# A transformer block on one Trainium2 core: the split of q and k for five pairs of heads in operations of 128 rows, with the halves put in place by transfers

## The chip, the core and the metric

The kernel runs on one core of a Trainium2 chip. A core has a matrix engine (TensorE, PE in the profile, with its weight loads as PEld), a vector engine (VectorE, DVE), a scalar engine (ScalarE, ACT), GpSimd (POOL) and SyncE (SP), which here only issues transfers. Each engine works through its own instructions in the order of the program; engines wait for each other by semaphores. Transfers (DMA) are issued by SP, ACT or POOL and run on 16 DMA engines. The metric is the time of one execution on the device in microseconds.

## The reference

One block for 512 tokens of width 1024: a gated feed-forward, a mixer of two kinds of attention, a second gated feed-forward, and a gated embedding, each with norms. Only the mixer's attention matters here:

```python
u = rms_norm(h, g_mix_pre[i])
qkv = u @ w_in[i]
q_a, k_a, v_a, q_b, k_b, v_b = jnp.split(
    qkv, np.cumsum([W_SB, W_SB, W_SB, W_CH, W_CH])[:5].tolist(), axis=-1)
o_a = stick_breaking_attention(split_heads(q_a, H_SB), split_heads(k_a, H_SB),
                               split_heads(v_a, H_SB))
o_b = chunk_band_attention(split_heads(q_b, H_CH), split_heads(k_b, H_CH),
                           split_heads(v_b, H_CH), rel_bias[i])
```

There are eight heads of each kind, of dimension 64. Both kinds begin with the scores, q times k transposed, for blocks of 128 queries.

## The kernel before

Every float32 product is made of rounded operands: a value x is split into a high half, which is x rounded to the matrix engine's float32r format (`act.copy`), and a low half, x minus the high half (`dve.tensor_tensor` with subtract). A product is then the sum of high x high, high x low and low x high. Weights arrive in raw tiles (`wr`, by SP's transfers, L187), are split into `wh` and `wl` (L313 on ACT, L314 on DVE), and are used by `mm3` (L248 to L250).

The mixer is one software pipeline. TensorE's order is written by hand: a loop over 64 steps (L1050), each of which takes one block of 128 queries of one head, makes its scores (`z`, L887 and L888), turns the weights of three steps ago (`pt`, L937, split into `th` and `tl`, L313 and L314) and multiplies those of five steps ago with v (`po`, L951 and L952). Between them `fill` puts a number of products from a list of work: the projections to q and k (`pj`, in `project`), to v (`pv`), and later of the output. The order on the other engines is chosen by the scheduler from its own costs. The raw weights of this part are fetched five chunks ahead of their split.

Heads go in pairs, s = 0 to 7; in this text a pair is named by that number (pairs 0 to 3 are of the first kind, 4 to 7 of the second; in the program's names pair 4 g + i has the suffix g i, so `qd010` is tile qd0 of pair 4). The projection of a pair gives q and k for 128 rows, 64 per head: `top` is the pair's first head, `bot` the second. `qk_out` (L815) makes from them three kinds of tiles, two of each (0 for the first head, 1 for the second), all of 128 rows by 512 tokens, so that the three products of the scores are done in two products over 128 rows:

- `qd0`, `qd1`: the high half of the head's q, twice, in top and in bot;
- `ks0`: k's high half of the first head in top, its low half in bot; `ks1`: the second head's low half in top, its high half in bot;
- `ql0`, `ql1`: q's low half in the head's own rows, zeros in the others (a memset by POOL, L824).

`z` is qd times ks plus ql times ks. Each kind of tile has two buffers, so pair s takes those of pair s - 2. Except for q of pairs 0 to 3 the projections' result is first multiplied on DVE by a norm factor into a scratch tile `qkf` (L830 for q, L832 for k), which lies in one buffer under the tag `t3`. Then, for q and k each, ACT casts the two heads with one operation of 64 rows each (L835), DVE subtracts with one of 64 rows each (L842), and for q ACT issues two transfers that copy the high half to the other 64 rows (L837). For k the low half is written by the subtraction straight into the other head's rows.

Pairs 0 and 1 are projected ahead of the loop; `PLAN` (L56) orders the rest. The second kind of attention adds a bias tile (`bi`, L915, by SP) to the scores (`zbc`, L922). The first kind makes `fa` and `be` on ACT (L900, L901), masks them on POOL (L903), and scans and multiplies them on DVE into `a` (L906, L907).

## Time and profile before

| | |
|---|---|
| median of 3 runs | 1002.78 us (1001.17 to 1005.86) |
| the profiled execution, its own time | 1002.25 us |
| its span, from the first to the last instruction | 1000.5 us |
| busy: PE, DVE, ACT, POOL | 980.4, 775.3, 585.8, 134.5 us |
| transfers of L837, ACT's queue | 16 of 128 KB, 3.0 us from issue to landing (median) |
| biases of L915, SP's queue | 8 of 256 KB, 2.7 us (median) |

Times in the rows of a profile count from the start of the span. A row of a timeline shows its start, its length, the engine and line, the operation, the tiles as written<-read, their shapes, how many were merged, and in brackets how long the engine stood idle before it and what ended that. The three products of `mm3` show as L248, L249 and L250. In the views of transfers a row ends with the size and the median time from issue to landing.

### The profile page before, as it was taken

How to read it: one execution, taken by the hardware profiler on the slowest of the kernel's cores; microseconds unless marked ns; L12 is line 12 of the kernel's file. 1: busy time of each engine (PE TensorE's matmuls, PEld its weight loads, DVE VectorE, ACT ScalarE, POOL GpSimd, SP SyncE). 2: the span in 40 equal slices, each digit the busy share in tenths (PEclk: the TensorE clock that was granted, in tenths of full speed). 3: DMA queues.
4: the chain of work that ended last, by engine and by line, in shares of the span. 5: the costliest groups of instructions: out<-in, count | busy, mean ns of one | idle time of the engine just before them, and what ended most of it. 6: DMA issues, size and time to landing. Idle time of an engine off the chain costs nothing.

```text
span 1000.5 us, 18453 instructions
## 1 busy us (share of the span) xinstructions
PE 980.4 (98%) x7242; PEld 922.5 (92%) x7242; DVE 775.3 (77%) x1357; ACT 585.8 (59%) x979; POOL 134.5 (13%) x221
## 2 busy tenths in 40 slices
PE   9999999999999999999999999999999999999996
PEld 7889999999999999888898899899999999999885
DVE  6777787677667788999999767796776787676857
ACT  6446654564455467777789655565643664555563
POOL 0001112122210004343000000011122122210000
PEclk9999999999999999999999999999999999999999
DMA  7348888988896132313332402269789888975202
GB/s 280 102 106 189 170 188 183 207 181 177 211 191 206 60 82 88 89 61 102 99 89 92 139 10 65 61 142 204 149 186 204 181 169 212 195 180 185 64 1 85
DMA packets 44855, 139.71 MB, mean 140 GB/s; under 512 B 5216, under 2 KB 5600, under 8 KB 44768
## 3 DMA queue, kind: packets, MB, share of 16 engines
q0 software_dynamic: 14976, 50.34, 30.5%
q1 hardware_dynamic: 28368, 85.83, 25.3%
q10 hardware_dynamic: 1424, 2.36, 0.9%
q8 instruction: 57, 0.93, 0.4%
q14 instruction: 30, 0.25, 0.1%
HBM read 134.31 MB, written 2.10 MB: 136 GB/s over the span
## 4 chain that ended last, share of the span: by engine, by line
PE 75%; DMA 8%; DVE 8%; ACT 4%; issue 4%; POOL 0%; SPq 0%; DVEq 0%; POOLq 0%; ACTq 0%
PE f_a L248 7%; PE f_a L250 7%; PE f_a L249 7%; PE f_c L248 3%; PE f_c L250 3%; PE f_c L249 3%; PE pj L248 3%; PE pj L249 3%; PE pj L250 3%; DMA wy<-in_wst_dram 3%; DVE wl L314 2%; PE pt L937 2%; PE f_d L250 2%; PE f_d L249 2%; PE f_d L248 2%
## 5 line engine op out<-in xcount | busy, mean ns | idle before, releaser
L314 DVE TENSOR_TENSOR wl<-wx,wh 128x1024 fp32r<-128x1024 f32 (+1 forms) x104 | 118.3, 1139 | 39.6 <-ACT wh L313 38.7
L313 ACT CAST wh<-wx 128x1024 fp32r<-128x1024 f32 (+1 forms) x104 | 101.8, 985 | 68.1 <-DMA wx<-in_wst_dram 37.4
L314 DVE TENSOR_TENSOR wl<-wr,wh 128x1024 fp32r<-128x1024 f32 (+2 forms) x100 | 109.3, 1099 | 28.8 <-ACT wh L313 28.1
L313 ACT CAST wh<-wr 128x1024 fp32r<-128x1024 f32 (+2 forms) x100 | 94.3, 950 | 46.0 <-DMA wr<-in_wgu_dram 14.0
L223 POOL DMA_DIRECT2D wx<-in_wst_dram x54 | 47.1, 872 | 403.8 <-DVE wl L314 339.5
L313 ACT CAST wh<-wy 128x1024 fp32r<-128x1024 f32 (+1 forms) x52 | 51.4, 988 | 47.5 <-DMA wy<-in_wdst_dram 23.7
L314 DVE TENSOR_TENSOR wl<-wy,wh 128x1024 fp32r<-128x1024 f32 (+1 forms) x52 | 59.2, 1139 | 15.8 <-ACT wh L313 15.2
L248 PE MATMUL pj<-um_hi,wh 128*128 128x512 f32 (+1 forms) x160 | 56.7, 355 | 1.2 <-DVE f_f L658 1.1
L249 PE MATMUL pj<-um_lo,wh 128*128 128x512 f32 (+1 forms) x160 | 55.7, 348 | 0.1
L250 PE MATMUL pj<-um_hi,wl 128*128 128x512 f32 (+1 forms) x160 | 55.8, 348 | 0.0
L248 PE MATMUL f_a<-f_U6h,wh 128*128 128x256 f32 x144 | 40.0, 278 | 2.0 <-DVE f_x L599 1.3
L248 PE MATMUL f_a<-f_U0h,wh 128*128 128x256 f32 x144 | 40.0, 278 | 0.0
L249 PE MATMUL f_a<-f_U0l,wh 128*128 128x256 f32 x144 | 39.8, 277 | 0.0
L250 PE MATMUL f_a<-f_U0h,wl 128*128 128x256 f32 x144 | 39.8, 277 | 0.0
L248 PE MATMUL f_b<-f_U1h,wh 128*128 128x256 f32 x144 | 39.8, 277 | 0.0
L249 PE MATMUL f_b<-f_U1l,wh 128*128 128x256 f32 x144 | 39.8, 277 | 0.0
L250 PE MATMUL f_b<-f_U1h,wl 128*128 128x256 f32 x144 | 39.8, 277 | 0.0
L248 PE MATMUL f_c<-f_U2h,wh 128*128 128x256 f32 x144 | 39.8, 277 | 0.0
L249 PE MATMUL f_c<-f_U2l,wh 128*128 128x256 f32 x144 | 39.8, 277 | 0.0
L250 PE MATMUL f_c<-f_U2h,wl 128*128 128x256 f32 x144 | 39.8, 277 | 0.0
L248 PE MATMUL f_a<-f_U5h,wh 128*128 128x256 f32 x144 | 39.8, 277 | 0.0
L249 PE MATMUL f_a<-f_U5l,wh 128*128 128x256 f32 x144 | 39.8, 277 | 0.0
(461 smaller groups left out, 3851.3 us busy)
## 6 DMA issues: line engine op xcount, KB each, us to landing
wx<-in_wst_dram POOLq DMA_DIRECT2D x54, 512.0 KB, 5.7
wx<-in_wst_dram SPq DMA_DIRECT2D x18, 512.0 KB, 4.9
wy<-in_wst_dram SPq DMA_DIRECT2D x18, 512.0 KB, 5.8
wr<-in_wst_dram SPq DMA_DIRECT2D x18, 512.0 KB, 5.8
wy<-in_wst_dram POOLq DMA_DIRECT2D x18, 512.0 KB, 5.8
wx<-in_wdst_dram POOLq DMA_DIRECT2D x24, 384.0 KB, 5.5
wr<-in_wqk_dram SPq DMA_DIRECT2D x16, 512.0 KB, 3.7
wr<-in_wgu_dram SPq DMA_DIRECT2D x15, 512.0 KB, 4.2
```

The costliest lines, as they stand in the source:

```text
L223: pool.dma_start(out=r, in_=block, accum_op=ALU.add)
L248: pe.matmul(ps, hi, mh, start=start, stop=False, skip_group_check=skip)
L249: pe.matmul(ps, hi, ml, start=False, stop=False, skip_group_check=skip)
L250: pe.matmul(ps, lo, mh, start=False, stop=stop, skip_group_check=skip)
L313: a = act.copy(hi, src)
L314: b = dve.tensor_tensor(lo, src, hi.bitcast(F32), ALU.subtract)
L937: pe.transpose(pt[:, qi * P:(qi + 1) * P], aw[qi][:, (j - qi) * P:(j - qi + 1) * P], ident[:])
```

## The change

For pairs 2 to 6 (`2 <= 4 * g + i < 7`), q and k are cast by one operation of 128 rows each, into qd0 or ks0 whole, and subtracted by one operation of 128 rows. The low half goes back into the scratch tile, or, for q of pairs 2 and 3, where the source lies in PSUM, into a new tile under the same tag `t3`. Then `move`, a transfer on SP's queue of 64 rows, puts the halves in place: for q five (the second head's high half into both halves of qd1, the first head's over the second's in qd0, the low halves into ql0 and ql1), for k three (the second head's high half to ks1, its low half to ks1, the first head's low half over the second head's high half in ks0). The two transfers on ACT's queue go for these pairs. Pairs 0, 1 and 7 are as before, and so are all products.

```diff
             for r, other in enumerate((bot, top)):
                 pool.memset(ql[r][other, :].bitcast(F32), 0.0)
+            def move(dst, src):
+                nc.sync.dma_start(out=dst.bitcast(F32), in_=src.bitcast(F32))
+
             for j, ps in enumerate(pss):
                 src = ps
                 if g or j:
...
                 dst = ks if j else qd
+                if 2 <= 4 * g + i < 7:
+                    a, b = dst
+                    act.copy(a[:], src[:])
+                    lo = (src if g or j else tmp(f"qlf{g}{i}", 3))[:].bitcast(F32R)
+                    dve.tensor_tensor(lo, src[:], a[:].bitcast(F32), ALU.subtract)
+                    move(b[bot, :], a[bot, :])
+                    move(b[top, :], lo[bot, :] if j else a[bot, :])
+                    move(a[bot, :], lo[top, :] if j else a[top, :])
+                    if j == 0:
+                        move(ql[0][top, :], lo[top, :])
+                        move(ql[1][bot, :], lo[bot, :])
+                    continue
                 for r, (own, other) in enumerate(((top, bot), (bot, top))):
                     act.copy(dst[r][own, :], src[own, :])
```

The order on TensorE and on GpSimd is the same before and after. On SyncE's queue, this is what stands between the projection weights and the biases around pair 4 before (`wr` with its chunk's number, `bi` with the head's):

```order
L187 DMA wr137_5605<-in_wqk_dram 128x1024
L187 DMA wr138_5737<-in_wqk_dram 128x1024
L187 DMA wr139_5842<-in_wo_dram 128x1024
L915 DMA bi0_5817<-in_bias_dram 128x512
L915 DMA bi1_5968<-in_bias_dram 128x512
```

And this after, where the moves of pair 4 (suffix 10) come among them:

```order
L187 DMA wr137_5611<-in_wqk_dram 128x1024
L826 DMA qd110_5696<-qd010_5695 64x512 x2
L187 DMA wr138_5745<-in_wqk_dram 128x1024
L826 DMA ql010_5697<-qkf100_5703 64x512
L826 DMA qd010_5695<-qd010_5695 64x512
L826 DMA ql110_5698<-qkf100_5703 64x512
L187 DMA wr139_5850<-in_wo_dram 128x1024
L826 DMA ks110_5700<-ks010_5699 64x512
L826 DMA ks110_5700<-qkf101_5712 64x512
L826 DMA ks010_5699<-qkf101_5712 64x512
L930 DMA bi0_5825<-in_bias_dram 128x512
L930 DMA bi1_5978<-in_bias_dram 128x512
```

The last move of q waits until the two into qd110 have landed, and ks010 is written only after the move that reads it has landed; the loads and biases behind them follow in that order.

On VectorE, these are the rows around k of pair 4 before (`qkf101` is the scratch tile of k, `a` and `tl` belong to the attention of pair 3):

```order
L832 TENSOR_TENSOR qkf101_5705<-pj101_5611,Rpre_77 128x512
L314 TENSOR_TENSOR wl134_5740<-wr134_5221,wh134_5739 128x1024
L309 TENSOR_TENSOR acc_76<-acc_76,o02_sq_5674 128x512
L906 SCALAR_TENSOR_TENSOR a071_5716<-fa71_5715 128x383
L314 TENSOR_TENSOR tl062_5731<-pt062_5726,th062_5730 128x384
L842 TENSOR_TENSOR ks010_5693<-qkf101_5705,ks010_5693 64x512
L907 TENSOR_TENSOR a071_5716<-a071_5716,be71_5714 128x383
L842 TENSOR_TENSOR ks110_5694<-qkf101_5705,ks110_5694 64x512
```

And after:

```order
L835 TENSOR_TENSOR qkf101_5712<-pj101_5617,Rpre_77 128x512
L314 TENSOR_TENSOR wl134_5748<-wr134_5227,wh134_5747 128x1024
L309 TENSOR_TENSOR acc_76<-acc_76,o02_sq_5680 128x512
L921 SCALAR_TENSOR_TENSOR a071_5724<-fa71_5723 128x383
L314 TENSOR_TENSOR tl062_5739<-pt062_5734,th062_5738 128x384
L841 TENSOR_TENSOR qkf101_5712<-qkf101_5712,ks010_5699 128x512
L922 TENSOR_TENSOR a071_5724<-a071_5724,be71_5722 128x383
```

One subtraction of 128 rows stands where the first of the two of 64 stood; the second is gone. The first row, the multiply of k, now waits until the moves that read q's low half from the scratch tile have landed.

## The prediction

> **What bounds the kernel now.** The change touches five of the eight pairs of heads, so I first looked at the stretch in which their projections and first scores run, from about 393 to 541 us, with the view of busy time by stretches (columns: length, then busy us and count for PE, weight loads, DVE, ACT, POOL, then granted clock, DMA share, GB/s).

> ```profile
> 393.00:541.00 148.00, 146.83 (x884) 129.16 (x883) 137.79 (x298) 118.99 (x251) 35.68 (x90) 1.00 0.32 93
> 393.00:433.90 40.90, 40.90 (x241) 35.92 (x241) 38.99 (x62) 32.55 (x66) 17.29 (x49) 1.00 0.32 90
> 436.00:476.00 40.00, 40.00 (x245) 35.39 (x244) 37.59 (x66) 30.11 (x60) 14.92 (x34) 1.00 0.30 82
> 479.00:541.00 62.00, 62.00 (x382) 55.04 (x380) 56.55 (x160) 52.50 (x118) 1.56 (x3) 1.00 0.35 102
> ```

> TensorE is without a gap in three of the four rows, at full clock. VectorE is close behind: 137.79 of 148 us. A busy PE can hide short stalls, so I asked next what PE waits for in this stretch, and then read its timeline at the places where two starts lie further apart than the same pair of rows does elsewhere.

> ```profile
> PE pt L937 <- DVE tl L314: 1.1, 1, 1.1
> ```

> ```profile
> 435.36 0.44 PE L937 MATMUL pt<-ident,a 128*128 128x128 f32 x2 [1.05 <-DVE tl L314]
> ...
> 476.85 0.40 PE L250 MATMUL pj<-um_hi,wl 128*128 128x512 f32 x1
> 477.20 0.33 PE L887 MATMUL z<-ks,qd 128*128 128x128 f32 x1
> 477.36 0.28 PE L888 MATMUL z<-ks,ql 128*128 128x128 f32 x1
> 477.76 0.30 PE L937 MATMUL pt<-ident,a 128*128 128x128 f32 x1
> ```

> One real wait, 1.05 us for a transpose that needs VectorE's split of an earlier one, and a small one at 477: from 476.85 to 477.76 pass 0.91 us. A 512-column product takes 0.23 us (469.96 to 470.19 below), a 128-column one by its columns an estimated 0.06, so the three need 0.35 and some 0.5 us are a stall. Together 1.6 us. **That is all that faster engines beside PE can give back here**: whatever VectorE and ScalarE save, PE has no more idle time to lose.

> **What is removed.** Per pair and per side (q, k) one 64-row cast on ScalarE, one 64-row subtraction on VectorE; per pair also two DMA issues on ScalarE's queue.

> ```profile
> L835 ACT CAST qd<-qkf x6: 617/618/622, 456.2 to 492.1; 64x512 fp32r<-64x512 f32 x6
> L842 DVE TENSOR_TENSOR ql<-qkf,qd x6: 674/682/690, 457.2 to 492.8; 64x512 fp32r<-64x512 f32 x6
> L832 DVE TENSOR_TENSOR qkf<-pj,Rpre x3: 672/685/693, 462.9 to 497.1; 128x512 f32<-128x512 f32 x3
> ```

> A 64-row operation takes 0.68 us and a 128-row one of the same length 0.69 us, so one operation of 128 rows is taken to cost what one of 64 did (bounds for the unseen 128-row split: 0.67 to 0.70). Ten subtractions less is 10 x 0.68 = 6.8 us of VectorE, ten casts less is 10 x 0.62 = 6.2 us of ScalarE. Nearly all of it lies beside a PE that never waits. It counts at two places.

> ```profile
> 432.60 1.40 DVE L842 TENSOR_TENSOR ks<-qkf,ks 64x512 fp32r<-64x512 f32 x2
> 434.04 0.69 DVE L906 TENSOR_TENSOR_SCAN a<-fa 128x255 f32<-128x255 f32 x1
> 434.64 0.66 DVE L314 TENSOR_TENSOR tl<-pt,th 128x512 fp32r<-128x512 f32 x1
> ```

> Ahead of the 1.05 us wait stand two subtractions of pair 3, a scan, and the split for which PE waits. With one subtraction less the split is done 0.70 us earlier: **-0.7 us** (0 if the scan then waits for something else, -1.05 at most).

> ```profile
> 474.50 1.39 DVE L842 TENSOR_TENSOR ql<-qkf,qd 64x512 fp32r<-64x512 f32 x2
> ```

> The same pair of subtractions of pair 5 stands a little ahead of the small wait at 477: **-0.5 us** (0 to -0.5).

> **What is added and moved.** Eight transfers of 128 KB a pair, 40 in all, on SyncE's queue, where they stand among the weight loads; ten on ScalarE's queue go. The bytes are few: the DMA share is 0.32 in this stretch. What counts is the order. A half that must go to the other 64 rows is now ready only after a transfer, and `a[bot]` may be overwritten only after the move that reads it has landed: for k that is cast, transfer, second transfer, one after the other. The nearest rows for one such transfer are the ones on ScalarE's queue, same size, SBUF to SBUF.

> ```profile
> DMA to landing us min/median/max: 2.2/2.3/5.5
> ...
> qd<-qd ACTq DMA_DIRECT2D x1, 128.0 KB, 4.0
> ```

> The first row is for the ten between 400 and 500 us; the second is one that was issued at 458.13, 0.83 us after a 512 KB load (457.30 below). So a hop takes 2.2 us on free engines, 4.0 behind a load, 5.5 at worst.

> Does the longer chain reach PE? The time between the multiply that opens the k side and the first score decides.

> ```profile
> 412.55 0.68 DVE L832 TENSOR_TENSOR qkf<-pj,Rpre 128x512 f32<-128x512 f32 x1
> ...
> 480.50 0.69 DVE L832 TENSOR_TENSOR qkf<-pj,Rpre 128x512 f32<-128x512 f32 x1
> ```

> ```profile
> 423.78 0.39 PE L887 MATMUL z<-ks,qd 128*128 128x512 f32 x1
> ...
> 494.53 0.39 PE L887 MATMUL z<-ks,qd 128*128 128x512 f32 x1
> ```

> Pair 2 has 11.2 us and pair 5 has 14.0 us; multiply 0.69, cast 0.62 and hops of 4.0 and 2.3 make 7.6, so both are covered, even with one hop at 5.5. Pairs 3 and 6 have longer still. **Pair 4 has not**:

> ```profile
> 462.85 0.69 DVE L832 TENSOR_TENSOR qkf<-pj,Rpre 128x512 f32<-128x512 f32 x1
> ...
> 466.81 0.69 DVE L842 TENSOR_TENSOR ks<-qkf,ks 64x512 fp32r<-64x512 f32 x1
> 467.52 0.56 DVE L907 TENSOR_TENSOR a<-a,be 128x383 f32<-128x383 f32 x1
> 468.12 0.69 DVE L842 TENSOR_TENSOR ks<-qkf,ks 64x512 fp32r<-64x512 f32 x1
> ```

> ```profile
> 461.91 1.05 ACT L313 CAST wh<-wr 128x1024 fp32r<-128x1024 f32 x1 [1.01 <-PE pj L249]
> ...
> 464.82 1.27 ACT L835 CAST ks<-qkf 64x512 fp32r<-64x512 f32 x2
> ```

> ```profile
> 457.30 0.33 SPq L187 DMA_DIRECT2D wr<-in_wqk_dram  x1
> 464.70 0.33 SPq L187 DMA_DIRECT2D wr<-in_wo_dram  x1
> 469.64 1.57 SPq L915 DMA_DIRECT2D bi<-in_bias_dram  x2
> ```

> ```profile
> 469.96 0.39 PE L887 MATMUL z<-ks,qd 128*128 128x512 f32 x1
> 470.19 0.40 PE L888 MATMUL z<-ks,ql 128*128 128x512 f32 x1
> ```

> The cast of k hardly comes earlier: ScalarE works through from 461.91, where it had waited for PE. It ends at 464.82 + 0.62 = 465.44. The load that the order puts just ahead of the first move goes out at 464.70, so that move stands as the one at 458.13 did: 465.44 + 4.0 = 469.4. The second move, which puts the low half of k into ks0, may go only then (its data is there at 467.5): 469.4 + 2.3 = 471.7. PE wants it at 469.96, and nothing else can pass it on PE: **+1.8 us** (bounds: hops of 2.2 and 2.2 give 469.84, nothing; 5.5 and 5.5 give 476.44, +6.5). The bias loads behind it go out at 469.64 as before, and are not what is late.

> A second new wait: the scratch tile of q (one buffer) is free for the k multiply only when two moves have read it. In pair 4 the last of them is issued at about 460.0 (cast end 456.8, one hop of 2.3, two issues) and lands, behind the load of 457.30, at about 462.5, against 462.85: I cost it at nothing, covered by that order; with a hop of 5.5 it would be 2.7 us, and VectorE's split for the next transposes would queue behind it. The weight loads behind the moves on SyncE's queue come some us later, which costs nothing: by the program's order the one of 464.70 is the fifth that ScalarE casts after 464.70, and that is at 511.75.

> ```profile
> 511.75 1.05 ACT L313 CAST wh<-wr 128x1024 fp32r<-128x1024 f32 x1 [0.39 <-PE pv L250]
> ```

> [...]

> **The sum**: -0.7 - 0.5 + 1.8 = +0.6 us on the profiled execution's 1002.25 us, that is 1002.9. The median shown is 1002.78, 0.5 above the profiled one; I add nothing for that.

> **Rivals.** (1) *Hops at their shortest*: both of pair 4's moves run as the median row, 465.44 + 4.6 = 470.04, stall 0.1; sum -0.7 - 0.5 + 0.1 = -1.1, or 1001.2. For it speaks the 2.3 median; against it the load issued 0.74 us earlier. [...] (2) *Slower: moves caught behind loads on SyncE's queue.* Both hops at 5.5 give +6.5, less 1.2 is +5.3: 1007.6; if the scratch wait of 2.7 us comes on top, some 1009. It decides once the two hops together exceed 10.7 us. For it: 5.5 was seen, beside a load and other copies. Against: after the first hop the load ahead has landed too, so the second hop should be free. (3) *Faster: VectorE is the true bound.* It is 93% busy; if its 6.8 us came off the end, 995.4. Against it: PE has only 1.6 us of gaps to give back.

> **How the numbers follow.** Forecast (a stall of 1 to 4 us at pair 4) 0.62; (1) 0.19; (2) 0.12, three quarters of it beyond +5 us; (3) 0.05; something outside these 0.02. A measurement of this kernel tells about 0.5% from no change, 5 us; so faster 0.05, same 0.85, slower 0.10. The range reaches from the largest gain without a stall (-1.05 - 0.5, 1000.7) to a second hop that is caught too (4.0 + 5.5, +3.8) with some of the scratch wait: 1000.6 to 1006.5.

> **What would show it.** In the profile after: PE's largest wait between 393 and 541 us is the first score of pair 4, for a DMA, 1 to 4 us; the wait at 435 shrinks by 0.7; ten subtractions of 0.69 us less on VectorE; the k multiply starts at once in pairs 2 to 6. It is wrong if PE waits for moves at another pair, if VectorE stands before a k multiply, or if PE's stretch shortens by more than 2 us.

## The result and the profile after

| | before | after |
|---|---|---|
| median of 20 runs each | 1001.22 us (997.59 to 1006.35) | 1007.54 us (1001.52 to 1013.13) |
| ratio, with its 95% interval | | 1.0061 [1.0045, 1.0076] |
| profiled execution: time, span | 1002.25, 1000.5 us | 1005.65, 1003.9 us |
| busy DVE, ACT | 775.3, 585.8 us | 768.0, 578.8 us |

The change makes the kernel slower by 0.6%, 4.5 to 7.6 us by the interval. (The ratios, here and below, are estimated for themselves and can differ from the quotient of the medians, by up to 0.0015.) The operations that it was to save are saved: VectorE is busy 7.3 us less and ScalarE 7.0. The groups of VectorE between 393 and 541 us of the kernel after show the price of a split of 128 rows (name, shapes and count, then total us and mean ns):

```profile
L841 DVE TENSOR_TENSOR qkf<-qkf,ks 128x512 fp32r<-128x512 f32 x5 | 3.4, 681 | 0.0
L841 DVE TENSOR_TENSOR qkf<-qkf,qd 128x512 fp32r<-128x512 f32 x3 | 2.0, 679 | 0.0
```

0.68 us, as one of 64 rows took. So the time went elsewhere. Runs of one kernel spread over 9 to 12 us, so I measure one stretch within the profiles: from the first product of pair 2's projection to the end of the last score. These are its first and last row in the timeline of TensorE, before and then after:

```profile
395.55 0.40 PE L248 MATMUL pj<-um_hi,wh 128*128 128x512 f32 x1
...
549.01 0.27 PE L888 MATMUL z<-ks,ql 128*128 128x128 f32 x1
```

```profile
398.33 0.40 PE L248 MATMUL pj<-um_hi,wh 128*128 128x512 f32 x1
...
502.31 0.39 PE L902 MATMUL z<-ks,qd 128*128 128x512 f32 x1
...
556.85 0.28 PE L903 MATMUL z<-ks,ql 128*128 128x128 f32 x1
```

The stretch is 153.7 us long before and 158.8 after: **+5.1 us, most of the loss and inside its interval**. By the first scores it arises at one place. From the stretch's start, pair 4's comes at 74.4 us before and 78.3 after (476.61, below), pair 5's at 99.0 and 104.0 (502.31, above), and from there on the difference stays at 5.0. So 3.9 us are lost by pair 4's first score, and a net 1.1 more between it and pair 5's. The waits of TensorE between 393 and 545 us (in total, times, longest), where before had a single kind of 1.7 us in all, and its timeline at pair 4:

```profile
PE z L902 <- DMA ks<-qkf: 2.8, 1, 2.8
PE pt L952 <- DVE tl L314: 1.6, 2, 1.1
```

```profile
470.96 0.22 PE L902 MATMUL z<-ks,qd 128*128 128x128 f32 x1
471.01 0.28 PE L903 MATMUL z<-ks,ql 128*128 128x128 f32 x1
471.79 0.30 PE L952 MATMUL pt<-ident,a 128*128 128x128 f32 x1 [0.50 <-DVE tl L314]
...
473.44 0.40 PE L250 MATMUL pj<-um_hi,wl 128*128 128x512 f32 x1
476.61 0.67 PE L902 MATMUL z<-ks,qd 128*128 128x512 f32 x1 [2.78 <-DMA ks<-qkf]
...
478.79 0.63 PE L248 MATMUL pj<-um_hi,wh 128*128 128x512 f32 x1
479.22 0.63 PE L249 MATMUL pj<-um_lo,wh 128*128 128x512 f32 x1
479.64 0.62 PE L250 MATMUL pj<-um_hi,wl 128*128 128x512 f32 x1
480.07 0.43 PE L248 MATMUL pj<-um_hi,wh 128*128 128x512 f32 x1
480.33 0.39 PE L249 MATMUL pj<-um_lo,wh 128*128 128x512 f32 x1
```

Three losses follow each other. A transpose waits for VectorE's split: 0.78 us from 471.01 to 471.79 where the score product needs about 0.12 (472.18 to 472.30 in the run with one added transfer, below), so 0.7. Then the first score of pair 4 waits for the last of k's moves: 3.17 us from 473.44, less 0.23 for the product, 2.9. Then the products come 0.43 us apart instead of 0.23 (480.07 to 480.33 is the step back): TensorE runs at half clock. The view by stretches shows that granted clock (the column after POOL):

```profile
476.00:481.00 5.00, 4.39 (x13) 3.49 (x14) 3.81 (x7) 2.73 (x4) 0.00 (x0) 0.66 0.47 137
```

A clock of 0.5 for 3.41 of these 5 us, as the trace's record of the granted clock has it from 476.7 on, gives the mean of 0.66, and costs 1.7 us of work. Of that the small stall of 0.5 that before had at 477 goes off. Why the score is late stands in the chain of work that leads to it (start, length, what):

```profile
463.71 3.98 DMA ql<-qkf
...
467.81 0.70 DVE qkf L835
...
470.09 4.19 DMA ks<-ks
474.28 0.02 issue
474.29 2.18 DMA ks<-qkf
476.47 0.14 issue
476.61 0.67 PE z L902
```

The lower half of it is the one that I forecast: cast, a hop of 4.19 behind a load, a hop of 2.18. The upper half is not: k's multiplication had to wait until the move of q's low half had landed. VectorE's timeline shows that wait in pair 3 and in pair 4:

```profile
432.80 0.69 DVE L835 TENSOR_TENSOR qkf<-pj,Rpre 128x512 f32<-128x512 f32 x1 [1.76 <-DMA ql<-qlf]
...
467.81 0.69 DVE L835 TENSOR_TENSOR qkf<-pj,Rpre 128x512 f32<-128x512 f32 x1 [2.08 <-DMA ql<-qkf]
```

And this is SyncE's queue ahead of it, with the times from issue to landing of the two moves of q's low halves of pairs 3 and 4:

```profile
459.83 1.29 SPq L826 DMA_DIRECT2D qd<-qd  x2
461.23 0.51 SPq L187 DMA_DIRECT2D wr<-in_wqk_dram  x1
461.85 0.47 SPq L826 DMA_DIRECT2D ql<-qkf  x1
463.14 0.46 SPq L826 DMA_DIRECT2D qd<-qd  x1
463.71 0.54 SPq L826 DMA_DIRECT2D ql<-qkf  x1
```

```profile
DMA to landing us min/median/max: 4.0/4.2/4.9
```

Two moves of q go out ahead of the weight load and push it back; the other three go out behind it and land late, 4.0 to 4.9 us after their issue. They land just behind the load: it lands at 466.18, they at 466.73, 467.23 and 467.69. With no weight load under way a hop took 2.18 us (the one of 474.29 above). The scratch tile is waited for a third time, in the other direction: the multiplication of pair 5's q stands 1.6 us until k's move has landed (476.60). With k's side alone, below, it stands 1.1 us and nothing is lost.

### The profile page after: what moved, and what is told of

Same layout as the page of the kernel before. It is cut to its first block, busy times and chain, and to the rows that moved or that the text cites. A ratio compares the mean times of both kernels' runs of the same rounds, so it can differ in the third digit from the quotient of the medians.

```text
span 1003.9 us, 18506 instructions
## 1 busy us (share of the span) xinstructions
PE 982.6 (98%) x7242; PEld 924.8 (92%) x7242; DVE 768.0 (76%) x1347; ACT 578.8 (58%) x969; POOL 135.4 (13%) x221
## 3 DMA queue, kind: packets, MB, share of 16 engines
q10 hardware_dynamic: 624, 1.05, 0.4%
## 4 chain that ended last, share of the span: by engine, by line
PE 79%; DVE 8%; DMA 6%; ACT 4%; issue 2%; SPq 0%; POOL 0%; DVEq 0%; ACTq 0%; POOLq 0%
PE f_a L248 8%; PE f_a L250 8%; PE f_a L249 8%; PE f_c L248 4%; PE f_c L250 4%; PE f_c L249 4%; PE pj L248 2%; PE pj L249 2%; PE pj L250 2%; PE f_b L248 2%; PE f_b L250 2%; PE f_b L249 2%; DMA wx<-in_wdst_dram 2%; PE f_d L249 2%; PE f_d L250 2%
## 5 line engine op out<-in xcount | busy, mean ns | idle before, releaser
L314 DVE TENSOR_TENSOR wl<-wx,wh 128x1024 fp32r<-128x1024 f32 (+1 forms) x104 | 118.3, 1139 | 44.1 <-ACT wh L313 43.1
L313 ACT CAST wh<-wx 128x1024 fp32r<-128x1024 f32 (+1 forms) x104 | 101.8, 984 | 67.0 <-DMA wx<-in_wst_dram 33.1
L314 DVE TENSOR_TENSOR wl<-wr,wh 128x1024 fp32r<-128x1024 f32 (+2 forms) x100 | 109.3, 1099 | 27.9 <-ACT wh L313 27.2
L313 ACT CAST wh<-wr 128x1024 fp32r<-128x1024 f32 (+2 forms) x100 | 94.4, 951 | 45.0 <-DMA wr<-in_wgu_dram 14.2
L313 ACT CAST wh<-wy 128x1024 fp32r<-128x1024 f32 (+1 forms) x52 | 51.3, 986 | 44.1 <-DMA wy<-in_wst_dram 19.4
L314 DVE TENSOR_TENSOR wl<-wy,wh 128x1024 fp32r<-128x1024 f32 (+1 forms) x52 | 59.2, 1138 | 13.7 <-ACT wh L313 13.6
L249 PE MATMUL pj<-um_lo,wh 128*128 128x512 f32 (+1 forms) x160 | 55.9, 349 | 0.1
L250 PE MATMUL pj<-um_hi,wl 128*128 128x512 f32 (+1 forms) x160 | 56.0, 350 | 0.0
L249 PE MATMUL f_a<-f_U5l,wh 128*128 128x256 f32 x144 | 39.9, 277 | 0.0
L250 PE MATMUL f_a<-f_U5h,wl 128*128 128x256 f32 x144 | 39.9, 277 | 0.0
L249 PE MATMUL f_c<-f_U2l,wh 128*128 128x256 f32 x144 | 39.9, 277 | 0.0
L250 PE MATMUL f_c<-f_U2h,wl 128*128 128x256 f32 x144 | 39.9, 277 | 0.0
L249 PE MATMUL f_a<-f_U6l,wh 128*128 128x256 f32 x144 | 39.9, 277 | 0.0
L249 PE MATMUL f_a<-f_U0l,wh 128*128 128x256 f32 x144 | 39.9, 277 | 0.0
L250 PE MATMUL f_a<-f_U0h,wl 128*128 128x256 f32 x144 | 39.9, 277 | 0.0
```

The costliest lines, as they stand in the source:

```text
L249: pe.matmul(ps, hi, ml, start=False, stop=False, skip_group_check=skip)
L250: pe.matmul(ps, lo, mh, start=False, stop=stop, skip_group_check=skip)
L313: a = act.copy(hi, src)
L314: b = dve.tensor_tensor(lo, src, hi.bitcast(F32), ALU.subtract)
```

## The experiments

Each was timed beside the kernel before on the same chip. "Stretch" is the length defined above, against 153.7 us; waits are of TensorE if not said otherwise. The run with one added transfer, in which no new wait appeared, had 153.69, so differences of a few tenths count as real here, as far as two profiles can tell; the medians tell some 2 us.

**Where: all pairs but pair 4.**

```diff
-                if 2 <= 4 * g + i < 7:
+                if 4 * g + i in (2, 3, 5, 6):
```

> The change for pairs 2, 3, 5 and 6, pair 4 as before. Theory A (the loss is pair 4's first score, which waits for k's moves, and the slower clock after that wait): no PE wait over 1.5 us between 393 and 541 us, the granted clock stays 1.00, and the time is that of the kernel before within 2 us. Rival B (every pair that is moved pays its share, through the wait of VectorE for the scratch tile or through the traffic): four of five parts of the loss stay, +5 us.

Measured: 1000.53 against 1001.74 us, 0.9993 [0.9969, 1.0018]; stretch +0.7. VectorE still waits 2.1 us for q's moves ahead of k's multiplication in pair 3, and TensorE's wait near 436 stays:

```profile
436.54 0.44 PE L952 MATMUL pt<-ident,a 128*128 128x128 f32 x2 [1.13 <-DVE tl L314]
```

So the four other pairs cost next to nothing, but they bring nothing either: at pair 3 the wait for the scratch tile eats the 0.7 us that the saved subtraction should have given. The loss needs pair 4.

**Where: pair 4 alone.**

```diff
-                if 2 <= 4 * g + i < 7:
+                if 4 * g + i == 4:
```

> The change for pair 4 alone. A: nearly all of the loss, +4 to +6 us, with one PE wait of 2 to 3 us for a DMA at the first score of pair 4 and a granted clock below 1.00 in the 25 us around it. B: a fifth of the loss, about +1.3 us.

Measured: 1003.84 against 1001.74 us, 1.0022 [1.0000, 1.0044]; stretch +3.0. The place is right, the size below the 4 to 6 us that I held likeliest, and the clock that I expected to fall did not in this profile.

```profile
476.12 0.47 PE L902 MATMUL z<-ks,qd 128*128 128x512 f32 x1 [2.77 <-issue]
476.43 0.39 PE L903 MATMUL z<-ks,ql 128*128 128x512 f32 x1
```

The same wait as in the full change, but the next product follows after 0.31 us, not 0.47, and the clock stays full. What is missing to +5.1 is mostly the clock: at the second score of pair 4 the full change is 2.0 us later than this run, only 0.4 of it before the first.

**Which wait: q's scratch tiles in buffers of their own.** Under the tag `t0` instead of `t3`, nothing in k's path waits for the moves of q; all else as changed.

```diff
-                    src = tmp(f"qkf{g}{i}{j}", 3)
+                    src = tmp(f"qkf{g}{i}{j}", 0 if j == 0 and 2 <= 4 * g + i < 7 else 3)
...
-                    lo = (src if g or j else tmp(f"qlf{g}{i}", 3))[:].bitcast(F32R)
+                    lo = (src if g or j else tmp(f"qlf{g}{i}", 0))[:].bitcast(F32R)
```

> The change, but the scratch tile of q in pairs 2 to 6 under the tag t0, so that the multiply of k need not wait for q's moves. A: the waits of 1.76 and 2.08 us on VectorE ahead of the k multiply of pairs 3 and 4 are gone; pair 4's first score waits 2 us less than the 2.78 us, that is 0.5 to 1.8 us, the clock stays at 1.00, and the time is within 2 us of before. Rival C (the two transfers one behind the other are the loss, the scratch tile is not): the wait stays above 2 us and the time 4 us or more above before.

Measured: 1000.94 against 1001.74 us, 0.999 [0.9963, 1.0016]; stretch -0.2. All waits of TensorE between 393 and 545 us:

```profile
PE z L902 <- DMA ks<-qkf: 1.1, 1, 1.1
```

One edit, of a tag, takes the whole loss away. What is left is the wait of pair 4's first score for k's two hops, and the wait near 435 is gone.

**Which half: q's side alone, k as before.**

```diff
-                if 2 <= 4 * g + i < 7:
+                if 2 <= 4 * g + i < 7 and j == 0:
```

> The change for q alone, k cast and subtracted in operations of 64 rows as before, so no transfer stands between k and the scores, but the scratch tile is still waited for. A: the k multiply of pair 4 waits some 2 us, pair 4's first score is late by 0 to 1.5 us, clock 1.00, time +0 to +2 us. Rival D (the wait of VectorE for the scratch tile alone makes the loss, by delaying the splits that PE needs): +4 us or more, with PE waits for VectorE and not for a DMA.

Measured: 1005.84 against 1001.74 us, 1.0055 [1.0027, 1.0083]; stretch +4.8. My own theory had 0 to 2 us here and fell, and rival D held: I had thought that without k's hops the scratch tile's wait is covered. It is not: VectorE stood still for 2.18 us ahead of k's multiplication in pair 3, and the rows behind it came late. Its timeline at pair 3, and TensorE's behind it:

```profile
436.55 0.69 DVE L835 TENSOR_TENSOR qkf<-pj,Rpre 128x512 f32<-128x512 f32 x1 [2.18 <-DMA ql<-qlf]
...
440.20 1.40 DVE L857 TENSOR_TENSOR ks<-qkf,ks 64x512 fp32r<-64x512 f32 x2
441.63 0.69 DVE L921 TENSOR_TENSOR_SCAN a<-fa 128x255 f32<-128x255 f32 x1
442.24 0.67 DVE L314 TENSOR_TENSOR tl<-pt,th 128x512 fp32r<-128x512 f32 x1
```

```profile
442.96 0.69 PE L952 MATMUL pt<-ident,a 128*128 128x128 f32 x2 [2.00 <-DVE tl L314]
...
444.30 0.41 PE L248 MATMUL pv<-wh,um_hi 128*128 128x256 f32 x1
...
446.41 0.28 PE L249 MATMUL pv<-wl,um_hi 128*128 128x256 f32 x1
```

The split `tl` for which TensorE waits comes behind the late multiplication and behind k's two subtractions of 64 rows, so the wait that was 1.05 us grows to 2.00. A stretch at half clock begins with it (256-column products at 0.41 us, then at 0.28), and at pair 4 two more waits of 0.5 and 0.7 us for the same split follow. Compared score by score with before, 3.7 of the 4.8 us are lost where k of pair 3 is made, and about 1 at pair 4, so this run loses its time at another place than the full change. In the full change one subtraction of k stands there and the wait is 1.13 us; that it is this which shields TensorE is argued from the two timelines.

**Which half: k's side alone, q as before.**

```diff
-                if 2 <= 4 * g + i < 7:
+                if 2 <= 4 * g + i < 7 and j == 1:
```

> The change for k alone, q as before, so nothing waits for the scratch tile and the k multiply of pair 4 starts at its old place. A: the two transfers one behind the other, the first behind a weight load, make pair 4's first score wait 1 to 2 us, the clock stays at 1.00, time +0 to +2 us. Rival C (two hops are the whole loss): wait over 2.5 us and +4 us or more.

Measured: 1000.44 against 999.98 us, 0.999 [0.9971, 1.0010]; stretch -0.2, and again one wait of 1.2 us at pair 4's first score. k's two hops in series, for themselves, cost what the saved subtractions give back.

**One hop for k, the scratch tile as changed.** ScalarE casts the second head's k once more, straight to its place, so that ks0's low half needs no first hop to land.

```diff
                     act.copy(a[:], src[:])
+                    if j:
+                        act.copy(b[bot, :], src[bot, :])
...
-                    move(b[bot, :], a[bot, :])
+                    if j == 0:
+                        move(b[bot, :], a[bot, :])
```

> The change, but k's high half of the second head is cast straight to its place by a second ScalarE operation of 64 rows, so that k needs one transfer after the other no longer (one hop in place of two, five casts more); the scratch tile as in the change. A: the k multiply of pair 4 still waits some 2 us, the first score of pair 4 waits 0 to 1.5 us, the clock stays 1.00, time within 2 us of before. B: +4 us or more.

Measured: 1003.54 against 999.98 us, 1.0023 [1.0007, 1.0039]; stretch +2.8. That lies between the two theories. The wait for the scratch tile stays (up to 2.5 us on VectorE), and TensorE waits at both places, at pair 4 longer than theory A allowed:

```profile
434.80 0.44 PE L955 MATMUL pt<-ident,a 128*128 128x128 f32 x2 [1.18 <-DVE tl L314]
...
471.59 0.47 PE L905 MATMUL z<-ks,qd 128*128 128x512 f32 x1 [1.93 <-DMA ks<-qkf]
```

TensorE's wait at pair 4's first score is thus 1.1 us with two hops and the scratch tile freed, 1.9 with one hop and the scratch tile as changed, 2.8 with both, and 0.7 with one hop and the tile freed (the next run). The scratch tile's wait is the larger part, 1.2 to 1.7 us, and the second hop the smaller, 0.4 to 0.9.

**Both mended: own buffers and one hop** (the edits of the two runs together).

> The second scratch tile and the single hop together. A: no wait at pair 4 over 0.7 us, the 1.05 us wait near 435 us shrinks by up to 0.7 us, time -1.5 to +0.5 us against before, which the measurement can hardly tell from none. B: +3 us or more.

Measured: 1000.42 against 999.98 us, 1.0006 [0.9982, 1.0031]; stretch -0.5. With nothing left of the new waits but 0.7 us at pair 4, VectorE is busy 8.6 us less than before and ScalarE 3.8, and the stretch gains half a microsecond. No version here beats the kernel before by more than its interval.

**The wait by itself: transfers added to the kernel before.** Pair 4's k tile is copied onto itself once, twice or three times in series ahead of its first score; nothing else is changed (N is 1, 2, 3).

```diff
+            for _ in range(N if 4 * g + i == 4 else 0):
+                nc.sync.dma_start(out=ks[0][bot, :].bitcast(F32), in_=ks[0][bot, :].bitcast(F32))
             return qd, ql, ks
```

> The kernel before with one added transfer of 128 KB (64 rows of pair 4's k tile onto themselves) between the last multiplication of pair 4's k and its first score, on SP's queue. Theory of the clock: a wait of TensorE of about 3 us is followed by 3.41 us at a granted clock of 0.5, a wait well below that is not. Then here: the first score of pair 4 waits 0 to 1.5 us, no stretch of granted clock at 0.5 beside it, and the time is +0 to +1.5 us against the kernel before. Rival (any hand-over through a transfer at this place upsets the clock): a stretch at 0.5 for 3.41 us also here, and +2 to +3 us.

> The kernel before, with two transfers of ks0's lower 64 rows onto themselves, one after the other, in pair 4 alone, and nothing removed: this measures what a late first score costs by itself. The transfers begin at about 467.5 and end at about 472.5, so PE waits about 2.5 us there. If a wait of this length also lowers the clock (theory A): the granted clock falls below 1.00 for some us after it and the loss is 1 to 2 us more than the wait, +3.5 to +5 us. If the wait costs only itself (rival E): +2 to +2.5 us and clock 1.00.

> As with one and with two added transfers, now three in series. Theory of the clock: the first score of pair 4 waits 5 to 6 us, the granted clock falls to 0.5 beside it for one stretch of 3.41 us or two, and the time is +5 to +8 us against the kernel before. Rival (a wait costs only its own length): +5 to +6 us and no stretch of low clock.

| added transfers | ratio | stretch | wait of pair 4's first score | half clock beside it |
|---|---|---|---|---|
| 1 | 0.9990 [0.9969, 1.0010] | 0.0 us | none | none |
| 2 | 1.0042 [1.0017, 1.0067] | +3.9 us | 2.96 us | 3.41 us |
| 3 | 1.0067 [1.0043, 1.0092] | +7.4 us | 5.44 us | 6.83 us |

The row of the wait with two and with three, each followed by the view by stretches from 475 to 480 us (with two, the profile puts the wait down to a cast that had long been done; with three, to the copies):

```profile
476.34 0.76 PE L889 MATMUL z<-ks,qd 128*128 128x512 f32 x1 [2.96 <-ACT qd L835]
```

```profile
475.00:480.00 5.00, 3.66 (x11) 2.96 (x12) 3.61 (x8) 2.74 (x5) 0.00 (x0) 0.66 0.65 206
```

```profile
476.33 0.77 PE L889 MATMUL z<-ks,qd 128*128 128x512 f32 x1 [5.44 <-DMA ks<-ks]
```

```profile
475.00:480.00 5.00, 3.67 (x10) 2.92 (x11) 1.20 (x4) 1.98 (x3) 0.00 (x0) 0.50 0.50 159
```

One hop cost nothing here, so the kernel before has slack for one and not for two. The waits of 2.96 and 5.44 us cost more than their length, +3.9 and +7.4 us of the stretch, with 3.41 and 6.83 us at half clock beside them. The theory that a wait costs only itself is out.

**The queue or the engines: q's low halves moved by POOL's queue.** All else as changed.

```diff
-                        move(ql[0][top, :], lo[top, :])
-                        move(ql[1][bot, :], lo[bot, :])
+                        for r, own in ((0, top), (1, bot)):
+                            nc.gpsimd.dma_start(out=ql[r][own, :].bitcast(F32), in_=lo[own, :].bitcast(F32))
```

> The changed kernel, with the two transfers of q's low halves out of the scratch tile issued by POOL, not by SP; all else as changed. Theory Q (the order within SP's queue holds them: they stand behind a weight load there and land after it): on POOL's queue, which has no load ahead of them, they land within 2.5 to 3 us of their issue, k's multiplication waits at most 0.8 us in pairs 3 and 4 (1.76 and 2.08 in the changed kernel), and the time is within 2 us of the kernel before. Rival S (the 16 DMA engines that they share with the load hold them, whatever the queue): they still take 4 us or more while the load runs, the wait stays near 2 us, and the time is +4 us or more.

Measured: 1005.99 against 1000.78 us, 1.0053 [1.0027, 1.0080]; stretch +5.5. The transfers issued between 459 and 466 us (KB each, median us to landing), those of pair 5, which had moves of q and a bias of 256 KB beside them but no weight load, from 497 to 503, and the multiplication of pair 4's k:

```profile
wr<-in_wqk_dram SPq DMA_DIRECT2D x1, 512.0 KB, 5.4
...
ql<-qkf POOLq DMA_DIRECT2D x2, 128.0 KB, 5.7
```

```profile
ql<-qkf POOLq DMA_DIRECT2D x2, 128.0 KB, 2.7
```

```profile
465.79 0.69 DVE L835 TENSOR_TENSOR qkf<-pj,Rpre 128x512 f32<-128x512 f32 x1 [1.83 <-DMA ql<-qkf]
```

On a queue with no load ahead of them the moves took even longer while the load ran, 5.7 us, and 2.7 us without one. At pair 4, where the time is lost, the order within SyncE's queue, my first reading, is therefore not what holds them. (At pair 3 the wait did fall, from 1.76 to 0.81 us, though the moves took 4.4 us there too.) What is left is the load itself: between 459 and 466 us the packets of SyncE's queue, the load among them, took 56.6% of the time of the 16 engines and those of POOL's 14.4%; the load landed at 464.61, and the two moves at 465.10 and 465.67. That the load holds them there is argued from these times: no run moved it out of the way.

## Why the prediction was wrong

I forecast 1002.9 us, no change, and a range up to 1006.5; measured were 1007.54, and +6 us against the kernel before.

- **The step that failed**: "I cost it at nothing, covered by that order", of the wait of k's multiplication for q's scratch tile. It rests on q's last move being issued at about 460.0 and landing at about 462.5, against 462.85. In the profile after it is issued at 463.71; the two runs are 3.0 us apart at pair 3's first score, so that is 460.7 by the clock of before, 0.7 late. And it took 3.98 us, not 2.5, for a reason that I had in hand: the load that I took to be ahead of it at 457.30 had itself been pushed behind two moves of q (461.23, or 458.2 by before's clock), and the three moves behind it took 4.0 to 4.9 us. I had moved the transfers and left the load where it was. The alternative that the prediction named for it, 2.7 us, was close to the 2.08 measured. VectorE stood before a k multiply, which the prediction had named as a sign of being wrong. With the scratch tile freed the loss is gone, so this step carries it, together with the two hops: with k's side alone they cost nothing, with one hop in place of two the stretch still loses 2.8 us.
- **The gain of 0.7 us near 435** did not come: the same wait at pair 3 (1.76 us on VectorE) made up for the saved subtraction. With the scratch tile freed it came.
- **The 1.8 us at pair 4** was right in mechanism and close in size: its hops were 4.19 and 2.18 us against 4.0 and 2.3, and the wait without the scratch tile's share is 1.1 us (q's tiles in buffers of their own) and 1.2 (k's side alone). So was its place: TensorE's largest wait is pair 4's first score for k's moves.
- **The clock was priced nowhere.** Behind the wait the granted clock fell to 0.5 for 3.41 us, some 1.7 us of work. It goes with the wait, not with the change: two copies added to the kernel before, with a wait of 2.96 us, have the same 3.41 us.
- **The rivals.** "Moves caught behind loads" had the right end, 1007.6 to 1009, and half of the way: neither hop was at 5.5, the scratch tile was it. Hops at their shortest did not happen, and VectorE as the true bound is excluded: with both new waits mended, the 8.6 us that VectorE is busy less bring nothing that the medians show.

How often the clock falls in the full change can be estimated, though each kernel has one profile. Every run has its mean granted clock on record: on average 0.9963 over the 20 runs of the change, 0.9978 over the 88 of the kernel before that stand beside the experiments. One drop of 3.41 us lowers it by 0.0017, so the change has about one drop per execution, some 1.5 us of its 6. Pair 4 alone has 0.9964, so its profile, in which the clock holds, is not its usual execution. The drop does not explain the wider spread (1001.5 to 1013.1): the fastest run has a clock of 0.997, the slowest 0.996. What does stays open. One microsecond between the stretch's 5.1 and the medians' 6 lies within their interval.

## What to carry to other kernels

The scratch tile here was free only when the transfer that read it had landed (467.69 us; VectorE began to write it next at 467.81), and VectorE stood still for 2.08 us with all that was queued behind: give a tile that is emptied by transfers its own buffer, or price its wait at the slow landing (4.0 to 4.9 us here). When transfers are put into a queue, move the loads behind them in the estimate too, and take the landing time beside a load, not the median (2.3). Operations saved on engines that ran beside a full TensorE could give back only TensorE's gaps, here 1.6 us, and one wait of 2.78 us there undid them, with 3.41 us at half clock on top.

## What the runs showed of the hardware

The penalty of a wait was not its length. In these profiles the granted clock fell to 0.5 for 3.41 us, or twice that, beside waits of 2.00 (q's side alone), 2.78 (the full change, with 0.50 shortly before), 2.80 (POOL's queue, 6.83 us of it), 2.96 and 5.44 us; it did not beside 1.9 us (one hop) nor beside 2.77 (the profile of pair 4 alone). The length alone does not decide.

```profile
473.30:476.71 3.41, 0.63 (x4) 0.23 (x3) 1.85 (x7) 1.11 (x2) 0.27 (x1) 1.00 0.51 113
```

```profile
471.03:474.44 3.41, 2.10 (x10) 1.46 (x9) 3.41 (x9) 1.94 (x4) 1.05 (x3) 1.00 0.56 178
474.44:477.85 3.41, 1.73 (x9) 1.45 (x10) 1.35 (x3) 0.71 (x2) 0.00 (x0) 1.00 0.64 192
```

TensorE is busy 0.63 of 3.41 us in the first, and half clock follows; cut as here, the wait of pair 4 alone is split over two, with 2.10 and 1.73 us of busy TensorE, and full clock stays. That the place of a wait within such a step makes the difference is my estimate from these two profiles and not shown. The place alone does not decide either: a wait of 1.82 us that ended at 260.03 us in the full change lies almost whole in one such step, 258.26 to 261.67, and the clock stayed at 1.00 from 255 to 270 us. Nor did the clock fall only at pairs 3 and 4: the profiled execution with POOL's queue has a mean granted clock of 0.991, against 0.998 before, and 6.83 us at half clock make only 0.0034 of the difference. What else counts stays open.
